# End of a feed-forward and entry of an attention mixer, taken in three token groups

## The chip, the cores and the metric

The kernel runs on one core of one Trainium2 chip. The metric is device time in microseconds (us) of one launch; less is better. Before the change three runs took 2756.0, 2763.02 and 2762.65 us, median 2762.65.

A core has five engines with queues of their own: TensorE (PE in the profile; PEld is its loading of weights), VectorE (DVE), ScalarE (ACT), GpSimd (POOL) and SyncE (SP), which here issues the transfers.

## The reference

Two layers, each a half feed-forward, a token mixer and another half feed-forward, over 512 latent tokens and 256 context tokens of width 1024. Every sub-layer modulates its input and closes with a layer norm of the weighted sum:

```python
def ffn_sublayer(h, shift, scale, gate, w_in, w_out, g, b):
    a, v = jnp.split(modulate(h, shift, scale) @ w_in, 2, axis=-1)
    return layer_norm(ALPHA * h + FFN_RES * gate * ((jax.nn.silu(a) * v) @ w_out), g, b)
# layer 1: first feed-forward (1a), then mixer 1 on u = modulate(h)
qkv = u_lat @ w_qkv                    # 16 query heads, 4 key and 4 value heads of 64
q, k = axial_rope(q) * scale, axial_rope(k)     # latent tokens only
kc, vc = u_ctx @ w_qkv[:, dq:]         # context: keys and values, no rotation
# softmax over a band of +-128 tokens, all context keys and a sink logit per head
```

Latent and context tokens have modulation vectors of their own. In layer 1 the context's output is not needed after mixer 1's keys and values.

## The kernel before

**Layout.** Activations are kept transposed: eight tiles (d = 0..7) of 128 features by 768 tokens, columns 0 to 511 latent (`NL`), 512 to 767 context. `z` is the residual, `uh` and `ul` are the modulated input as a high and a low part, so that a product of near single precision is three matmuls: `mm3` (L162) does high x high, low x high and high x low. Weights are loaded as 256 KB quarters of a unit (`wunit`, L122), and split likewise: the high part by an ACT cast (L102), the low part by a POOL subtraction (L104). They lie in a ring of eight pairs of tiles (`RING`), a unit taking four; the feed-forward's last downs lie in slabs of their own.

**Norms.** `ln` (L1303) makes a list of steps for one group of tokens: `sums`, `mean`, `centers`, `variance`, `spreading`, `out` and `kept`. The first three add the eight tiles on VectorE and POOL, have TensorE take the mean over features, subtract it (L364), square on ACT and add again; `variance` and `spreading` compute the reciprocal root (L354 to L359) and spread it over the partitions with TensorE. `out` (`mods`, L484) normalises each tile (L480) and modulates it in `mod_out` (L299): ACT writes `uf` (L317), ACT or VectorE writes the high part `uh` (L319, L321), VectorE subtracts for `ul` (L322). `kept` (`keep`, L324) scales `z` for the residual on POOL (L329, L335). The latent tokens lie in column order of the grid until a norm with `rm=True` writes them in row order; that was `l3`, the norm behind 1a, whose high part, low part and kept tile go through permuted views.

**Order.** A norm's steps are called at named points of other work: `plan(point=steps)` files them, and `at(point)` in the loops runs them there. That is the order of the program; the framework (`schedule_with_timeline_sim=True`, L1511) then fixes each engine's own order when the kernel is built, by what a simulated timeline has ready. `behind(x, y)` adds an order by hand.

**End of 1a** (`ffn`, from L786). `av` is an up product: a and v, 48 matmuls for a group of tokens, then silu, product and split (L522 to L525). `down` adds eight tiles of 48 matmuls to `z` (L495). The last unit's products go: latent up, latent down of the unit before, latent up, latent down; then the same for the context (256 columns), with the latents' norm beside it; the context's norm only begins at the end.

**Entry of mixer 1** (`wa_mixer`, L1103). Values of four latent token tiles (`v_tiles`, L872, tile vw), keys (wk), each rotated by `rope` (a matmul with a rotation matrix, prk, and three elementwise operations) and stacked in halves by `stack_k` (L859); then queries (wq, prq) for the first two head groups, the context's keys (wkc), and the context's values, for which the values' weights are loaded a second time (tiles with _b). Meanwhile the context's norm is made. Then the attention: scores (sw, sc), exponentials (pw, pc), transposes (tpw, tpc) and outputs (wo).

## Time and profile before

| | |
|---|---|
| profiled execution, its own time | 2773.53 us |
| its span | 2771.7 us |
| mean granted TensorE clock | 0.985 |
| TensorE (PE) busy | 96% |
| VectorE (DVE) / ScalarE (ACT) / GpSimd (POOL) busy | 67% / 43% / 60% |
| read from HBM | 300.92 MB, 113 GB/s over the span with what is written |

How to read the rows below. A row of busy time by stretches has the stretch, its length, then for PE, PEld, DVE, ACT and POOL the busy time with the number of instructions, then the granted TensorE clock (1.00 is full), the share of the DMA engines and GB/s. A row of waits names who waited for whom: total us, times, longest. A row of instructions has its start, its duration, engine, line, operation, what it writes and reads, the shapes and how many were merged; brackets hold the idle time before it and what ended it. A row of groups has the count behind x, then the busy time and the mean of one in ns, then idle time before. TensorE overlaps its matmuls, and their ends are modelled, so the distance of starts is its pace.

### The profile page before, as it was taken

Reading aid. Unit: us, or ns where it says so; the run is one execution under the profiler, and the core shown is the slowest. Engines: PE = TensorE matmul, PEld = TensorE weight load, DVE = VectorE, ACT = ScalarE, POOL = GpSimd, SP = SyncE. Lnnn points to the kernel's source line nnn. Section 1 sums busy time; section 2 is a strip of 40 time slices with the busy share of each in tenths; the row PEclk is TensorE's granted clock in tenths of the full one; section 3 lists DMA queues with packets and bytes.
Section 4 is the critical chain, followed back from the end, with each engine's and each line's share of the span. In section 5 each row is a group of like instructions: output and inputs, shape, how many; then the busy total and the mean of one; then the engine's idle time right before and its main releaser. Section 6 shows DMA issues by size and latency. Waiting matters only on the chain. (4 is left out here: it accounts for less than half of the span.)

```text
span 2771.7 us, 47917 instructions
## 1 busy us (share of the span) xinstructions
PE 2659.9 (96%) x16954; PEld 2423.5 (87%) x16954; DVE 1857.4 (67%) x4250; ACT 1204.9 (43%) x2493; POOL 1674.3 (60%) x1522
## 2 busy tenths in 40 slices
PE   8999999999999989999999999999998999899997
PEld 5899998888888889999998899999986777898997
DVE  4877777775555677656565776666587667677765
ACT  5334343366446344343433434343336655444442
POOL 4786765464434556867664577767545445667762
PEclk9999999999999999999999999999998999999998
DMA  9367555422222213444453236465722111235551
GB/s 320 105 174 205 143 155 152 144 80 61 58 58 57 63 46 92 117 127 126 125 132 106 73 87 165 112 166 165 205 87 63 32 31 47 63 103 126 133 143 57
DMA packets 295615, 311.92 MB, mean 113 GB/s; under 512 B 27856, under 2 KB 193872, under 8 KB 294352
## 3 DMA queue, kind: packets, MB, share of 16 engines
q1 hardware_dynamic: 278960, 279.36, 33.8%
q0 software_dynamic: 16128, 29.37, 6.3%
q8 instruction: 134, 2.20, 0.3%
q14 instruction: 105, 0.86, 0.1%
q10 hardware_dynamic: 288, 0.14, 0.0%
HBM read 300.92 MB, written 12.25 MB: 113 GB/s over the span
## 5 line engine op out<-in xcount | busy, mean ns | idle before, releaser
L104 POOL TENSOR_TENSOR wl<-wr,wh 128x512 fp32r<-128x512 f32 x200 | 262.7, 1332 | 161.2 <-ACT wh L102 102.7
L104 POOL TENSOR_TENSOR wl_s<-S,wh_s 128x512 fp32r<-128x512 f32 x240 | 316.6, 1354 | 53.5 <-ACT wh_s L102 53.0
L102 ACT CAST wh_s<-S 128x512 fp32r<-128x512 f32 x256 | 155.9, 620 | 430.3 <-POOL S L636 151.2
L636 POOL TENSOR_TENSOR S<-wr,wr 128x512 f32<-128x512 f32 x128 | 173.6, 1356 | 191.8 <-DMA wr<-in_wst_dram 177.5
L211 DVE CUSTOM_DVE_ANT_0 jk<-wt,cb 128x512 f32<-128x512 f32 x360 | 244.5, 679 | 23.7 <-DMA wt<-in_wmodt_dram 18.9
L104 POOL TENSOR_TENSOR wl_a<-wr,wh_a 128x512 fp32r<-128x512 f32 x144 | 189.5, 1364 | 17.9 <-ACT wh_a L102 14.0
L102 ACT CAST wh_a<-wr 128x512 fp32r<-128x512 f32 x192 | 118.9, 622 | 152.8 <-PE pd1b L165 21.8
L102 ACT CAST wh<-wr 128x512 fp32r<-128x512 f32 x200 | 120.3, 617 | 85.5 <-DMA wr<-in_wst_dram 21.9
L495 DVE SCALAR_TENSOR_TENSOR z<-pd0b,gt,z 128x256 f32<-128x256 f32 (+1 forms) x168 | 97.0, 594 | 43.9 <-PE pd0b L166 43.2
L495 DVE SCALAR_TENSOR_TENSOR z<-pd1a,gt,z 128x512 f32<-128x512 f32 (+1 forms) x160 | 95.5, 613 | 39.1 <-PE pd1a L166 38.5
L912 POOL TENSOR_SCALAR p<-p,l 128x512 f32<-128x512 f32 x64 | 44.5, 697 | 110.0 <-DVE l L1020 107.5
L495 DVE SCALAR_TENSOR_TENSOR z<-pd0a,gt,z 128x512 f32<-128x512 f32 (+1 forms) x160 | 93.4, 611 | 16.5 <-PE pd0a L166 16.3
L335 POOL TENSOR_SCALAR z<-z,ag_None,ab_None 128x256 f32<-128x256 f32 (+1 forms) x78 | 62.7, 807 | 63.7 <-DVE uh L321 48.8
L636 POOL TENSOR_TENSOR S<-wr,S 128x512 f32<-128x512 f32 x64 | 90.4, 1413 | 3.5
L636 POOL TENSOR_TENSOR S<-S,wr 128x512 f32<-128x512 f32 x64 | 90.3, 1411 | 2.9
L912 POOL TENSOR_SCALAR pw<-pw,l 128x512 f32<-128x512 f32 (+1 forms) x64 | 41.2, 643 | 66.7 <-DVE l L1214 25.7
L1019 ACT ACTIVATE p<-s,m 128x512 f32<-128x512 f32 x64 | 44.0, 689 | 81.2 <-DVE m L1017 76.5
L317 ACT ACTIVATE ufl<-z,bi_None,sc_None 128x256 f32<-128x256 f32 (+1 forms) x86 | 55.3, 654 | 52.9 <-DVE z L480 51.8
L322 DVE TENSOR_TENSOR ul<-ufl,uh 128x256 fp32r<-128x256 f32 (+1 forms) x88 | 61.0, 699 | 5.1 <-ACT uh L319 3.6
L495 DVE SCALAR_TENSOR_TENSOR z<-pd1b,gt,z 128x512 f32<-128x512 f32 (+1 forms) x91 | 53.2, 618 | 11.2 <-PE pd1b L166 10.4
L211 DVE CUSTOM_DVE_ANT_0 jk<-zspare,cb 128x512 f32<-128x512 f32 x88 | 59.7, 678 | 0.5
L163 PE MATMUL vn<-wh,uh 128*128 128x256 f32 x192 | 54.9, 286 | 1.0 <-DVE nq L856 0.5
(1483 smaller groups left out, 10650.8 us busy)
## 6 DMA issues: line engine op xcount, KB each, us to landing
wr<-in_wst_dram SPq DMA_DIRECT2D x456, 256.0 KB
wt<-in_wmodt_dram SPq DMA_DIRECT2D x206, 256.0 KB
zspare<-in_wmodt_dram SPq DMA_DIRECT2D x50, 256.0 KB
wr_0b<-in_wst_dram SPq DMA_DIRECT2D x47, 256.0 KB
wr_1b<-in_wst_dram SPq DMA_DIRECT2D x47, 256.0 KB
wr_2b<-in_wst_dram SPq DMA_DIRECT2D x47, 256.0 KB
wr_3b<-in_wst_dram SPq DMA_DIRECT2D x47, 256.0 KB
wm<-in_wmod_dram SPq DMA_DIRECT2D x8, 1024.0 KB
```

The costliest lines, as they stand in the source:

```text
L102: nc.scalar.copy(hi[:], src[:])
L104: x = eng.tensor_tensor(out=lo[:], in0=src[:], in1=hi[:].bitcast(F32), op=ALU.subtract)
L163: behind(nc.tensor.matmul(ps, a[0], b[0], start=first, stop=False), in_front[0])
L211: x = nc.vector.tensor_tensor_reduce(out=junk[:], in0=w[:], in1=cb[st], scale=1.0, scalar=0.0, op0=ALU.mult, op1=ALU.add, accum_out=out[st])
L317: nc.scalar.activation(uf[:, :n], zs, AF.Identity, scale=s1, bias=s2)
L322: return hi, nc.vector.tensor_tensor(out=lo, in0=uv, in1=uo.bitcast(F32), op=ALU.subtract)
L335: nc.gpsimd.tensor_scalar(out=zs, in0=zs, scalar1=prm[2][:, d:d + 1], scalar2=prm[3][:, d:d + 1], op0=ALU.mult, op1=ALU.add)
L495: last[0] = nc.vector.scalar_tensor_tensor(out=zt(d, c0, c1), in0=pd, scalar=gt[:, d, st:st + 1], in1=zt(d, c0, c1), op0=ALU.mult, op1=ALU ...
L636: nc.gpsimd.tensor_tensor(out=t[:], in0=a[:], in1=b[:], op=o)
L912: nc.gpsimd.tensor_scalar(out=p, in0=p, scalar1=r, scalar2=0.0, op0=ALU.mult, op1=ALU.add)
L1019: last_exp[0] = nc.scalar.activation(p[:], ps[:], AF.Exp, bias=m[:, 0:1], scale=-1.0, accum_out=l[:, 0:1])
```

## The change

- The downs and ups at the end of 1a go by three groups, `w3`: context first, then the two halves of the latents (256 columns each). Context up, latent up, context down of the unit before, context up, context's last down; then latent down, latent up, and the latents' last down in two halves. Weights are loaded as before.
- The norm `l3` has three groups of 256 columns. Its steps are planned under the latents' downs, and from there at points named wa in the mixer's entry.
- The mixer's entry makes values and keys tile by tile: for each group and each d the six matmuls of the values and the six of both key tiles, as inputs come. Values of a group share a bank, and so do the context's keys; `opener` lets only the first matmul of a bank start it, with the others ordered behind. The second load of the values' weights is gone. Keys are rotated once all groups are through, between and behind the first two query projections; `rope` is cut in `scaled` and `turned`, and uses a bank of "s" instead of "mm".
- Row order is written by `l2`, the norm before 1a, instead of `l3`, and the tile that it leaves free serves from then on as a buffer for the modulation weights (`spare`); there only `uf` and the kept tile go through permuted views.
- In norms of over 256 columns, and in `l3` and `l4`, ACT writes the high part of all eight tiles as a copy of `uf` (before: five tiles on ACT from `z`, three on VectorE).

```diff
     def mod_out(nm, d, c0, c1, st, prm, rm=False, dd=None):
-        uo, uv, lo, zv = uh[d][:, c0:c1], uf[:, :n], ul[d][:, c0:c1], zs
+        uo, uv, lo = uh[d][:, c0:c1], uf[:, :n], ul[d][:, c0:c1]
         if rm:
-            uo, uv, lo, zv = rowm(uo), rows(uv), rowm(lo), rows(zs)
-        nc.scalar.activation(uf[:, :n], zs, AF.Identity, scale=s1, bias=s2)
-        if nm[:2] == "l4" or d in (1, 2, 4, 5, 7):
-            hi = nc.scalar.activation(uo, zv, AF.Identity, scale=s1, bias=s2)
+            nc.scalar.activation(rowm(uv), rows(zs), AF.Identity, scale=s1, bias=s2)
         else:
-            hi = nc.vector.tensor_scalar(out=uo, in0=zv, scalar1=s1, scalar2=s2, op0=ALU.mult, op1=ALU.add)
+            nc.scalar.activation(uv, zs, AF.Identity, scale=s1, bias=s2)
+        if n > 256 or nm[:2] in ("l3", "l4"):
+            hi = nc.scalar.copy(uo, uv)
+        elif d in (1, 2, 4, 5, 7):
+            hi = nc.scalar.activation(uo, zs, AF.Identity, scale=s1, bias=s2)
+        else:
+            hi = nc.vector.tensor_scalar(out=uo, in0=zs, scalar1=s1, scalar2=s2, op0=ALU.mult, op1=ALU.add)
...
     def ffn(...):
+        if parted:
+            x0, x1, x2 = parted
+            ws = [wunit(again=u)]
+            av(ws[0], "l_0", x0, *gl[0], None, 4)
+            av(ws[0], "l_0", a, *gl[0], None, 4)
+            tick()
+            wd = [wunit("L", again=u - 1)]
+            down(wd[0], f"{NCH - 2}", gs, x0, True)
+            ws.append(wunit(again=u + 1))
+            av(ws[1], "l_1", x0, *gl[1], None, 4)
...
+            wd.append(wunit("L", again=u + 2))
+            down(wd[1], "l", gl, x0, True)
+            for f in post(0):
+                f()
+            down(wd[0], f"{NCH - 2}", gs, a, True)
+            av(ws[1], "l_1", a, *gl[1], None, 4)
+            down(wd[1], "l", gl, x1, True)
+            for f in post(1):
+                f()
+            down(wd[1], "l", gl, x2, True)
+            for f in post(2):
+                f()
+            return
...
     def wa_mixer(gt):
-        iv = wpos[0]
-        vt = v_tiles("w", wunit(), range(4), ("mm", "c"))
-        w = wunit()
...
+        for gi, (c0, c1, _) in enumerate(w3):
+            for k in range(DT):
+                u = [t[k] for t in (uh, ul)]
+                x = None
+                for j in range(2):
+                    x = mm3(vp[gi][:, j * 256:(j + 1) * 256], [t[:, c0 + j * P:c0 + (j + 1) * P] for t in u],
+                            kw(wv, k, 0, 256), k == 0, k == DT - 1 and j == 1, None if k else x)
+                x = None
+                for i in range(2):
+                    x = mm3(kp[i][:, c0:c1] if gi else kc[:, i * NC:(i + 1) * NC], kw(w, k, i * P, i * P + P),
+                            [t[:, c0:c1] for t in u], k == 0, k == DT - 1 and (i == 1 or gi > 0), None if k or gi else x)
+                at(f"wa{gi}_{k}")
...
+            if gi == 0:
+                for i in range(2):
+                    stack_k(*ks[i], NL, NT, kc[:, i * NC:(i + 1) * NC])
+        kes = [scaled(f"k{i}", kp[i], 1.0) for i in range(2)]
...
+        qes = [query(0, wq, 0)]
         for i in range(2):
-            ps = bank("mm", f"wkc{i}")
-            mmk(ps[:, :NC], w, i * P, NL, NT)
-            stack_k(*ks[i], NL, NT, ps[:, :NC])
-        vt += v_tiles("w", wunit(again=iv), range(4, 6), ("mm", "c"))
+            stack_k(*ks[i], 0, NL, turned(f"k{i}", kes[i]))
+        qes.append(query(0, wq, 1))
+        qs = [stacked_q(f"q0_{i}", qes[i]) for i in range(2)]
...
-    l2 = [ln("l2", i, g, 0, 2, 1, 0, "o", firm=i == 0) for i, g in enumerate(g2)]
-    l3 = [ln("l3", i, g, 1, 0, 1, 3, "o", True, firm=i == 0, alone=i == 1) for i, g in enumerate(g2)]
+    l2 = [ln("l2", i, g, 0, 2, 1, 0, "o", True, firm=i == 0) for i, g in enumerate(g2)]
+    w3 = g2[1:] + g1
+    l3 = [ln("l3", i, g, 1, 0, 1, 3, "oto"[i], held=i < 2) for i, g in enumerate(w3)]
...
-    plan(vw_3=l3[1][1:3], wk1=l3[1][3:4], wq0_0=l3[1][4:6] + l3[0][6:] + l3[1][6:])
+    plan(pd1a_9_0_3=l3[0][1:3], pd1a_9_0_7=l3[0][3:4], pa1a_l_1_0=l3[0][4:6], pv1a_l_1_0=l3[0][6:],
+         pd1a_l_256_3=l3[1][1:3], wa0_2=l3[1][3:4], wa0_4=l3[1][4:6], wa0_6=l3[2][1:3],
+         wa1_2=l3[2][3:4], wa1_5=l3[2][4:6], wa1_7=l3[1][6:], wa2_7=l3[2][6:])
```

67 lines of the change are left out of this document (42 added, 25 removed).

## The prediction

> **What bounds the kernel now.** I read the head of the page first, then busy time by stretches around the change, then TensorE's waits there, then single instructions.
>
> ```profile
> span 2771.7 us, 47917 instructions
> PE 2659.9 (96%) x16954; PEld 2423.5 (87%) x16954; DVE 1857.4 (67%) x4250; ACT 1204.9 (43%) x2493; POOL 1674.3 (60%) x1522
> ```
>
> TensorE is busy 96% of the span; only about 112 us are idle in all, so a change of order can win only where TensorE waits, or where its clock is down. The stretches show where that is:
>
> ```profile
> 2060.00:2080.00 20.00, 15.57 (x108) 13.74 (x106) 19.95 (x27) 13.38 (x15) 13.91 (x9) 1.00 0.00 1
> 2080.00:2100.00 20.00, 18.02 (x79) 14.69 (x80) 15.53 (x38) 6.15 (x15) 7.84 (x6) 0.83 0.23 59
> 2100.00:2120.00 20.00, 15.55 (x67) 11.97 (x66) 16.35 (x31) 17.73 (x32) 10.37 (x10) 0.91 0.05 14
> ```
>
> From the end of 1a's downs to the start of mixer 1's attention TensorE has 15 to 18 us of work in each 20, while VectorE is full in the first stretch (19.95 of 20). Who is late, from TensorE's waits between 2064 and 2148 us (the smallest three left out):
>
> ```profile
> PE vw L166 <- DVE ul L322: 4.7, 4, 1.9
> PE prq L1119 <- ACT qeq L1117: 3.9, 1, 3.9
> PE sw L1175 <- ACT pw L1200: 3.0, 3, 1.5
> PE vw L163 <- DVE uh L321: 1.2, 1, 1.2
> PE tpw L893 <- DVE wkl L864: 1.2, 1, 1.2
> PE vw L165 <- POOL wl_2b L104: 1.0, 1, 1.0
> PE vw L165 <- POOL wl_1b L104: 0.6, 1, 0.6
> ```
>
> These make 15.6 us: waits for the latent tokens' modulated tiles (4.7 and 1.2), for the queue of rotations (3.9), for the values' weights loaded a second time (1.6), for the context's stacked keys (1.2), and the filling of the attention (3.0). And the clock fell three times after such waits:
>
> ```profile
> 2082.00:2088.00 6.00, 5.11 (x23) 5.11 (x24) 5.40 (x10) 1.36 (x3) 2.05 (x2) 0.50 0.25 76
> 2109.00:2113.00 4.00, 3.56 (x7) 2.21 (x8) 2.84 (x7) 3.95 (x8) 2.19 (x3) 0.57 0.00 0
> 2140.00:2147.00 7.00, 6.21 (x26) 4.90 (x27) 5.38 (x16) 5.00 (x19) 3.40 (x5) 0.52 0.44 112
> ```
>
> Busy time multiplied by what the clock lacks (5.11 x 0.50, 3.56 x 0.43, 6.21 x 0.48) is 2.6 + 1.5 + 3.0 = 7.1 us. So about 22.7 us are lost between 2064 and 2148; that is the pot.
>
> **What the change does, part by part.** *Narrower matmuls.* The latent half of the last down and the latent keys go in two groups of 256 columns.
>
> ```profile
> 2031.11 0.39 PE L163 MATMUL pd1a_l<-gh1a_l,wh_2b 128*128 128x512 f32 x1
> 2031.34 0.39 PE L165 MATMUL pd1a_l<-gl1a_l,wh_0b 128*128 128x512 f32 x1
> 2050.15 0.28 PE L165 MATMUL pd1a<-gl1a,wh_0b 128*128 128x256 f32 x1
> 2050.27 0.28 PE L166 MATMUL pd1a<-gh1a,wl_0b 128*128 128x256 f32 x1
> ```
>
> What counts is the distance of the starts: 0.226 us at 512 columns (over a long run of rows), 0.12 us at 256. Two halves cost 0.24, so each pair adds 0.014. The down has 8 x 6 = 48 such matmuls and the keys 2 x 24 = 48: 96 pairs, +1.3 us on TensorE, which is the path. The Trainium skill ("TensorE: Matmul & The Clock Gate", Back-to-back issue gap) has a start-to-start of N/2.4 + 2.5 ns; by that a pair would add 2.5 ns and the whole 0.24 us. The trace has about 10 ns more for each matmul, so I keep 1.3.
>
> *Ends of the downs.* Today a whole down of other tokens lies between the last gated tile of 1a and its use. Now the context's last up product is followed at once by the down that reads it, and so is the latents'. The way from the last up matmul to the split tile is four operations:
>
> ```profile
> 2047.41 0.39 ACT L522 ACTIVATE sl1a_l<-pa1a_l 128x256 f32<-128x256 f32 x1
> 2050.23 0.43 DVE L523 TENSOR_TENSOR pv1a_l<-pv1a_l,sl1a_l 128x256 f32<-128x256 f32 x1
> 2011.65 1.33 POOL L104 TENSOR_TENSOR wl_3b<-wr_3b,wh_3b 128x512 fp32r<-128x512 f32 x1
> ```
>
> With the two that follow, of the same size, that is 1.6 us for the context, and (by width) some 2.6 for the latents. The first halves of the sums (i=0, three matmuls of 0.12 each, in the four or so free banks: 1.4 us) cover most of it. I take 0.8 us, ends 0 and 2.5. The weights are there: the last unit's split on POOL ended at 2013 us (third row), and the new order needs it at about 2024. Their loads keep their order on SP's queue; the moved steps issue no others.
>
> *The norm of the latents.* Today it is one norm of 512 columns whose output is permuted to row order while it is split. The same operations at the entry of 1a are not permuted:
>
> ```profile
> L322 DVE TENSOR_TENSOR ul<-ufl,uh 128x512 fp32r<-128x512 f32 x8 | 14.0, 1752 | 0.0
> L319 ACT ACTIVATE uh<-z,bi_None,sc_None 128x512 fp32r<-128x512 f32 x5 | 6.7, 1341 | 0.0
> L329 POOL TENSOR_SCALAR z<-z,ag_None,ab_None 128x512 f32<-128x512 f32 x7 | 13.0, 1851 | 3.0 <-DVE uh L321 2.6
> L322 DVE TENSOR_TENSOR ul<-ufl,uh 128x512 fp32r<-128x512 f32 x8 | 6.7, 838 | 0.0
> L317 ACT ACTIVATE ufl<-z,bi_None,sc_None 128x512 f32<-128x512 f32 x8 | 6.5, 814 | 11.3 <-DVE z L480 11.3
> L335 POOL TENSOR_SCALAR z<-z,ag_None,ab_None 128x512 f32<-128x512 f32 x8 | 9.5, 1198 | 0.0
> L102 ACT CAST wh<-wr 128x512 fp32r<-128x512 f32 x200 | 120.3, 617 | 85.5 <-DMA wr<-in_wst_dram 21.9
> ```
>
> The first three rows are 2060 to 2085, the next three 1534 to 1556, the last the whole span. The lower parts alone take VectorE 14.0 us against 6.7. In the new order the permutation is gone from here and VectorE loses the three high parts too, which is why the first wait (5.9 us) and its slow clock (2.6) should go. Instead there are three small norms. The context's, 256 columns wide today, shows the size:
>
> ```profile
> 2090.46 2.74 DVE L364 TENSOR_TENSOR z<-z,pml 128x256 f32<-128x256 f32 x8 [1.57 <-PE pml L442]
> 2097.65 0.17 DVE L472 TENSOR_SCALAR pvl<-pvl 128x2 f32<-128x2 f32 x1 [0.70 <-PE pvl L467]
> 2108.24 0.75 DVE L480 TENSOR_TENSOR z<-z,prl 128x256 f32<-128x256 f32 x2
> 2058.21 0.17 DVE L472 TENSOR_SCALAR pvl<-pvl 128x4 f32<-128x4 f32 x1 [1.26 <-PE pvl L467]
> 2062.26 1.27 DVE L480 TENSOR_TENSOR z<-z,prl 128x512 f32<-128x512 f32 x2
> L317 ACT ACTIVATE ufl<-z,bi_None,sc_None 128x256 f32<-128x256 f32 x8 | 4.6, 593 | 0.1
> ```
>
> From centring to the root's start are 7.2 us. From there to the first normalised tile it took 10.6 us, but among the rotation's work; the latents' own (fourth and fifth row) took 4.1. A first split tile is then four operations of 0.4 to 0.6 us, 2 us. With 2 us of sums that is 15.5 us. The context's norm lies under the latents' downs and up product (2 x 48 x 0.226 + 2 x 48 x 0.12 = 33 us) and costs nothing; without that cover it would be these 15.5 us. The first latent group's lies under the other group's down (48 x 0.12 = 5.8) and the context's values and keys (96 x 0.12 = 11.5): 17.3 us, hidden with 1.8 to spare. The second group has 11.5 us more cover, but its centering stands behind the first group's output on VectorE and its squares behind it on ACT (8 tiles x two operations of 0.59 = 9.4 us). So it is centred while the first group's tiles are made, starts its additions when they end, and has its first tile some 10 us later, while TensorE needs 11.5 us for the eight tiles: I work out 0 to 4 us of wait and take 2.0; at the far end, 7 (the contended 10.6 in place of 4.1). TensorE's order has the small matmuls of a norm in it, so such a wait holds all that is queued behind it, the keys' matmuls above all.
>
> *Entry of the mixer.* The second load of the values' weights goes (four 256 KB transfers on SP's queue, four casts, four POOL subtractions), with the 1.6 us waited for it; the context's keys are stacked early, which takes the 1.2. But the values' and keys' weights now hold all eight pairs of the ring until the last group, so the query's weights can be split only as that group's tiles pass; the last quarter is needed 4 us behind the group (six tiles x 0.68) and takes about 2 (cast 0.6, POOL 1.3): nothing, if POOL isn't behind with the two keeps; else up to 2. Both query projections (24 x 0.226 = 5.4 us each) now stand before the queries are rotated, and those of the context, today's filler at that point (first and last row below; the third is the attention's first output), are done.
>
> ```profile
> 2117.36 0.28 PE L163 MATMUL vw<-wh_0b,uh 128*128 128x256 f32 x1
> 2134.41 0.28 PE L166 MATMUL vw<-wh_3b,ul 128*128 128x256 f32 x1
> 2147.81 0.44 PE L903 MATMUL wo<-pw,vtw 128*64 128x128 f32 x4
> ```
>
> So after the last query TensorE has nothing but rotations (about 1 us) until one is added and stacked: I take 2.5 us, ends 0 and 6 (ACT's stack of keys and queries in one row). Then the attention fills as today: 3.0 of wait and 3.0 of slow clock stay, ends 2 and 10, since that filler is missing.
>
> *Entry of 1a.* The permutation moves here. ACT makes all eight tiles: a permuted one of 1.34 and a copy of 0.8 or less, with four casts of 0.6 about 19 us in all, against 21.7 us that TensorE needs for the 96 matmuls of 512 that read them. So it stays just ahead. POOL's keeps cost 8 x (1.85 - 1.20) = 5.2 us more, and the context's sums are queued behind them there; VectorE is relieved of three operations. TensorE's waits there today:
>
> ```profile
> PE pa1a L163 <- DVE uh L321: 1.0, 1, 1.0
> PE pa1a L165 <- DVE ul L322: 0.8, 2, 0.6
> ```
>
> I take 1.5 us more, ends -1.8 (they vanish) and +5 (the whole delay of POOL). In the other norms of 512 columns the high part also goes from VectorE to ACT in three tiles of eight: three operations of 0.81 (fifth row of the groups above) change their engine beside TensorE's work. I take nothing; uncovered it would be 2.4 us to either side.
>
> *The sum.* Lost today 22.7 us. Kept or new: 1.3 + 0.8 + 2.0 + 2.5 + 3.0 + 3.0 + 1.5 = 14.1. Left are 8.6, and 0.7 of the small waits that the rows above leave out go too: -9.3 us. The profiled execution took 2773.53 us (1.8 around its span) and becomes 2764.2. The runs shown have their median 0.4% lower, at 2762.65, and 0.4% of nine microseconds is nothing: **2753.4 us**.
>
> **Rivals.** *A, the entry's end takes the gain.* The values' and keys' matmuls were already issued tile by tile as the inputs came (the timeline shows vw and wk by turns from 2065), so only the shorter norms help, and what they win is given back waiting for the stacked queries and in an attention that fills without filler: 6 in place of 2.5, 10 in place of 6, and 4 for the second group. That is 9 us worse: no change, 2762. For it: ACT is busy 17.73 of 20 us at 2100 to 2120 with just these stacks. Against: keys and context are complete earlier, and two of today's three slow stretches come before.
>
> The Trainium skill (same page, The HAM clock gate) says that an idle window of about 3.4 us halves the clock and a busy one of that length restores it. By that rule a wait for the second group of 2 us leaves the clock alone, and only the query's wait with the fill halves it once: my single 3.0. The rows agree in the half (0.50), though 2082 came after three waits of 1.1 to 1.9 us and no whole idle window.
>
> *B, the norms queue one behind the other: slower.* If the second group's centring does not start until the first group's output is through, and each chain takes as long as the context's did (17.8 us from centring to the first normalised tile), then the first group, centred at 2062, has its first split tile at 2082, 4.5 us after TensorE wants it; it ends at 2093.5; the second is centred at 2092 and has its first tile at 2112, 18.5 us late: 23 us lost where I have 2. Against the 9.3 gained that is 12 us slower: 2774.5. It decides from 11 us of waiting before the groups (no gain); from 20 the loss is measurable. For it: VectorE was full (19.95 of 20) in this place with one norm, and now has two chains in a row. Against: ACT's 9.4 us leave VectorE gaps in which the second group can centre.
>
> *C, everything hides.* The queries' rotation is drawn into the second projection and the groups never wait: 2.0 + 2.5 + 3.0 + 1.5 more, -18: 2744.
>
> **How the numbers follow.** About 0.3%, 8 us, is what a measurement of this kernel can tell from no change. Forecast 0.58 (of which 0.44 beyond 8 us and 0.14 inside), A 0.20, B 0.12, C 0.10. Faster 0.44 + 0.10 = 0.54, same 0.14 + 0.20 = 0.34, slower 0.12. The range takes C and the good ends below, A with the entry of 1a at its worst above (+5 or so): 2742 to 2769; B stays out. The forecast's own range is 2746 to 2759.
>
> **What would show it.** Right: no wait of vw for ul above 1 us in the first two groups, no second load of the values' weights, clock at 1.00 until the first scores, the last query matmul near 2117 us and the first wo near 2132 (2147.8 today), lower parts of 0.4 us. The entry of 1a keeps its waits within 3 us, with POOL's keeps at 1.3 to 1.9 us. Wrong: waits above 4 us before a group's first tile (B); or the first wo near 2145 with the gap before it (A); or a loss of over 3 us between 1535 and 1660.

## The result, and the profile after

The changed kernel is slower: ratio to the kernel before 1.0073, 95% interval 1.0048 to 1.0098, which is 20 us (13 to 27) on the 2759.32 us that the kernel before took as median of the runs beside it. The median of the changed kernel's four runs is 2783.99 us.

The profiled execution of the changed kernel is the lowest of its runs (2773.63 us), the one of before lies 14 us above the median of its kernel (2773.53). So the two spans are nearly equal by chance, and the traces have to be compared by stages. First the head of the page after:

```profile
span 2771.8 us, 48164 instructions
PE 2651.6 (96%) x17052; PEld 2423.0 (87%) x17052; DVE 1839.1 (66%) x4282; ACT 1210.4 (44%) x2528; POOL 1668.4 (60%) x1536
```

The stages are cut at four marks of TensorE, the same in all kernels: start of the last down matmul of 0b (pd0b_l), of the last matmul of the background product p61a, which is the last before the changed end of 1a, of the first and of the last attention output of mixer 1 (wo). In us:

```
                    pd0b_l    p61a      first wo  last wo   last prfin
before              1536.42   1993.31   2147.81   2355.04   2759.09
changed             1522.87   1982.40   2148.27   2362.46   2759.08
length before                  456.9     154.5     207.2     404.1
length changed                 459.5     165.9     214.2     396.6
```

The change costs 2.6 us in 1a with its entry, 11.4 at the end of 1a and the mixer's entry, and 7.0 in the attention: 21 us, as the timed runs say. Only these three lengths are used below. Outside them the trace of before is the slower one: it is 13.5 us behind at the first mark, and its 1b takes 404 us, against 395 to 402 in the changed and trial kernels. Of the 13.5, 7.3 arise between the first and the last matmul of the background product p60a in 0a (344.9 us in before, 337.6 in the changed kernel). The change does nothing there, and e3 below, which is the changed kernel in that place, takes 343.5: that is a difference between executions. The rest lies in part where the change acts (the first modulation and the norms of 512 columns ahead of the mark have all high parts from ScalarE too); with one trace of before it stays open whether some of it is a gain of the change. The marks p61a and first wo in the trace of the changed kernel:

```profile
1982.40 0.33 PE L169 MATMUL p61a<-uh,wl_a 128*128 128x384 f32 x1
2148.27 1.09 PE L940 MATMUL wo<-pw,vtw 128*64 128x128 f32 x16
```

The stretches of the changed kernel that answer to those shown of before (columns: stretch, then busy time and count of TensorE, weight loads, VectorE, ScalarE, GpSimd, then granted clock, share and GB/s of the transfers):

```profile
2060.00:2080.00 20.00, 9.93 (x68) 8.93 (x67) 12.72 (x42) 8.78 (x24) 6.76 (x10) 0.78 0.03 7
2080.00:2100.00 20.00, 16.90 (x118) 16.25 (x118) 13.66 (x44) 12.00 (x29) 7.49 (x13) 0.80 0.01 1
2100.00:2120.00 20.00, 19.00 (x122) 16.64 (x121) 8.43 (x15) 10.31 (x23) 15.47 (x15) 1.00 0.38 107
2120.00:2140.00 20.00, 11.81 (x40) 7.78 (x38) 16.32 (x20) 15.04 (x25) 9.67 (x7) 0.73 0.20 52
```

VectorE is relieved, as intended (12.72 in place of 19.95), but TensorE has only 9.93 us of work in the first 20, at a lower clock. What it waits for between 2064 and 2148 us:

```profile
PE pvl L475 <- DVE aql L355: 6.9, 1, 6.9
PE prq L1160 <- ACT qeq L1154: 4.7, 1, 4.7
PE sw L1235 <- ACT pw L1260: 4.5, 2, 2.9
PE vw L164 <- ACT uh L324: 3.0, 1, 3.0
PE pml L450 <- DVE yl L367: 1.8, 1, 1.8
PE prl L403 <- DVE yl L367: 1.3, 1, 1.3
PE wq L164 <- ACT qek L1154: 1.0, 1, 1.0
PE sw L1235 <- DVE wq L893: 0.6, 1, 0.6
```

The first, fourth, fifth and sixth row are one stall, in front of the first latent group's first value matmul: 13.0 us. TensorE's and GpSimd's instructions there, in order of time:

```profile
2054.19 1.09 POOL L343 TENSOR_SCALAR z<-z,ag_None,ab_None 128x256 f32<-128x256 f32 x2 [10.72 <-ACT ufl L322]
2059.40 0.91 POOL L355 TENSOR_TENSOR asl<-zspare,z 128x256 f32<-128x256 f32 x1
2061.24 1.76 POOL L355 TENSOR_TENSOR asl<-asl,z 128x256 f32<-128x256 f32 x2
2066.25 0.59 PE L450 MATMUL pml<-asl,onesd 128*128 128x256 f32 x2
2067.15 0.28 PE L169 MATMUL wkc<-uh,wl 128*128 128x256 f32 x1
2074.37 1.02 PE L475 MATMUL pvl<-onesd,aql 128*128 128x1 f32 x4 [6.94 <-DVE aql L355]
2083.85 0.58 PE L164 MATMUL vw<-wh,uh 128*128 128x256 f32 x1 [2.96 <-ACT uh L324]
```

The group's last accumulation ends at 2048.3 us, its sums (asl) are done at 2063.9, their mean is taken at 2066.3, one microsecond before the context's keys (wkc) end, and almost everything after that is a wait.

### The profile page after: what moved, and what is told of

Read it like the earlier page. It is cut to its first block, busy times and chain, and to the rows that moved or that the text cites. A ratio compares the mean times of both kernels' runs of the same rounds, so it can differ in the third digit from the quotient of the medians.

```text
span 2771.8 us, 48164 instructions
## 1 busy us (share of the span) xinstructions
PE 2651.6 (96%) x17052; PEld 2423.0 (87%) x17052; DVE 1839.1 (66%) x4282; ACT 1210.4 (44%) x2528; POOL 1668.4 (60%) x1536
## 4 chain that ended last, share of the span: by engine, by line
PE 53%; DVE 7%; ACT 2%; DMA 2%; issue 1%; POOL 1%; SPq 0%; DVEq 0%; ACTq 0%; POOLq 0%
PE pd0b L164 2%; PE pd0b L168 2%; PE pd0b L169 2%; PE pd1a L168 2%; PE pd1a L164 2%; PE pd1a L169 2%; PE wo L940 1%; PE pd1b L164 1%; PE pd1b L168 1%; PE pd1b L169 1%; DVE z L503 1%; DMA wr<-in_wst_dram 1%; PE tpw L930 1%; DVE z L372 1%; PE wq L164 0%
## 5 line engine op out<-in xcount | busy, mean ns | idle before, releaser
L503 DVE SCALAR_TENSOR_TENSOR z<-pd1a,gt,z 128x512 f32<-128x512 f32 (+1 forms) x150 | 88.0, 606 | 34.1 <-PE pd1a L169 26.8
L343 POOL TENSOR_SCALAR z<-z,ag_None,ab_None 128x256 f32<-128x256 f32 (+1 forms) x84 | 57.0, 682 | 68.6 <-DVE uh L328 36.8
L168 PE MATMUL vn<-wl,uh 128*128 128x256 f32 x192 | 54.3, 283 | 0.0
```

Source lines behind the costliest of these rows:

```text
L168: nc.tensor.matmul(ps, a[0], b[1], start=False, stop=False)
L343: nc.gpsimd.tensor_scalar(out=zs, in0=zs, scalar1=prm[2][:, d:d + 1], scalar2=prm[3][:, d:d + 1], op0=ALU.mult, op1=ALU.add)
L503: last[0] = nc.vector.scalar_tensor_tensor(out=zt(d, c0, c1), in0=pd, scalar=gt[:, d, st:st + 1], in1=zt(d, c0, c1), op0=ALU.mult, op1=ALU ...
```

## The experiments

Stage lengths less those of before (456.9, 154.5 and 207.2), and the timed ratios with their intervals:

```
kernel                                 1a     to first wo  attention  ratio
changed                               +2.6    +11.4        +7.0       1.0073 [1.0048, 1.0098]
e1  no scaling of the context         +2.6     +6.5        +8.3       1.0037 [1.0019, 1.0055]
e2  context's norm earlier            +2.1    +11.6        +6.6       1.0055 [1.0040, 1.0069]
e3  rotation in its former bank       +1.8    +11.0        +0.8       1.0034 [1.0017, 1.0051]
e4  row order alone (on before)       +2.3     -8.4        +0.5       0.9982 [0.9962, 1.0001]
e5  own buffer for the sums           +1.9     +7.6        +8.1       1.0021 [1.0008, 1.0034]
e6  five places mended                +1.9     +8.0        -0.3       1.0023 [1.0008, 1.0038]
e7  row order alone, highs shared     +4.2     -9.0        +0.2       0.9942 [0.9923, 0.9960]
e8  earlier and own buffer            +3.3    +11.1        +2.1       1.0035 [1.0017, 1.0054]
e9  as e4, again                      +2.8     -8.3        +0.2       0.9956 [0.9942, 0.9971]
e10 no context norm                   +4.2     -2.7        +9.1       1.0022 [1.0008, 1.0036]
e11 e4, first query scaled on VectorE +2.9    -10.5        +0.1       0.9972 [0.9957, 0.9988]
e12 e10, bank, later centring         +3.7     +2.8        +1.8       1.0028 [1.0016, 1.0041]
```

e4 and e9 are the same kernel, and their lengths differ by 0.5 us at most. The lengths of 1a differ more, from +1.8 to +4.2, among kernels in which it is the same. All of them hang on the one trace of before, and for most kernels they add up to more than the timed loss: in e5 to 17.6 us, where the ratio says 6, in e1 to 17.4 for 10; e9 gains 5.3 us by the lengths and 12 by the ratio. So several microseconds lie outside the three stages, as said above, and a ratio does not confirm a length by itself.

Four theories of the 13 us were tried: GpSimd's order (1), too much work on VectorE and ScalarE (2), ScalarE's stacking between the squares (3), and, from e1 on, the buffer of the sums (4).

**e1.** The context's kept tiles leave the plan:

```diff
-    plan(pd1a_9_0_3=l3[0][1:3], pd1a_9_0_7=l3[0][3:4], pa1a_l_1_0=l3[0][4:6], pv1a_l_1_0=l3[0][6:],
+    plan(pd1a_9_0_3=l3[0][1:3], pd1a_9_0_7=l3[0][3:4], pa1a_l_1_0=l3[0][4:6],
```

> The changed kernel without the eight operations on POOL that scale the context's residual after its norm (left out of the computation: the context's residual keeps its unscaled value; nothing on the path waits for it). Theory 1 (POOL, in its order, has these eight ahead of the sums of the first latent group's norm, so that the sums wait until about 2063 us though their inputs are there at about 2050): the sums come about 8 us earlier, the mean matmul of the first latent group at about 2058 instead of 2066, the 13 us of waits before its first tile fall to 3 to 5 us, the first wo comes near 2139 instead of 2148.3, and the time is 8 to 10 us below the changed kernel's, level with the kernel before within 3 us. Theory 2 (VectorE and ScalarE have too much to do there, whatever the order): the first wo stays within 2 us of 2148. Theory 3 (ScalarE's stacking of the context's keys stands between the squares of the norm): the mean matmul comes early, but the first tile by less than 4 us earlier, since the wait for the variance grows instead.

Measured: first wo 4.9 us better. But the sums, with GpSimd empty, still began late, and the mean came only 0.9 us earlier by the marks (this trace runs 6.3 us ahead at p61a), the group's first value 1.4; the other 3.5 us were gained behind the queries' rotation. The first of the sums, and the mean:

```profile
2050.58 0.74 POOL L355 TENSOR_TENSOR asl<-zspare,z 128x256 f32<-128x256 f32 x1 [13.40 <-DVE ul L329]
2059.02 0.59 PE L450 MATMUL pml<-asl,onesd 128*128 128x256 f32 x2
```

GpSimd idles for 13.4 us and is released by a lower part (ul) of the context, of which the sums read nothing. It is the ring: `total` takes its two tiles from the six buffers of `t2`, which the context's eight unsplit tiles (`uf`) hold since the change, because they no longer have the buffers of the mixer's phase. Theory 1 is wrong in the size that it gave; theory 4 follows, and e5 tests it.

**e2.** Mean of the context's norm ahead of the next product, root and output at earlier points:

```diff
...
+            if firm == 2:
+                in_front[0] = x
...
-    plan(pd1a_9_0_3=l3[0][1:3], pd1a_9_0_7=l3[0][3:4], pa1a_l_1_0=l3[0][4:6], pv1a_l_1_0=l3[0][6:],
+    plan(pd1a_9_0_5=l3[0][1:3], pa1a_l_1_0=l3[0][3:4], pv1a_l_1_0=l3[0][4:],
```

> The changed kernel with the context's norm drawn forward: its mean matmul stands ahead of the next product of the latents' downs, and its root and its output are put one or two plan points earlier. Theory 1 (the context's norm is drawn out from 2020 to 2054 us by its place in TensorE's order and by being mixed with the latents' downs, and its operations on POOL then delay the first latent group): the context's mean matmul at about 2026 instead of 2032, POOL's scaling of the context over by about 2055 instead of 2061, waits before the first group's first tile 13 to about 7 us, first wo near 2142. Theory 2 (too much work on VectorE and ScalarE): the first wo stays within 2 us of 2148, the earlier work only comes in the way of the latents' sums. If the sums on VectorE that stand behind the background's products set the mean, the mean matmul stays at about 2030 and the gain is under 3 us.

Measured: nothing gained (+11.6). The context's scale factors were spread 4.8 us earlier (first row below against 2052.38 in the changed kernel, with the traces 4.8 apart at p61a), but the first group's waits only changed their place:

```profile
2042.78 0.61 PE L403 MATMUL prl<-idn,yl 128*128 128x128 f32 x4
2071.63 1.19 PE L450 MATMUL pml<-asl,onesd 128*128 128x256 f32 x2 [3.06 <-DVE pvl L366]
2077.19 1.20 PE L403 MATMUL prl<-idn,yl 128*128 128x128 f32 x4 [4.37 <-DVE yl L367]
```

**e3.** One word:

```diff
-            pr = bank("s", f"pr{nm}")
+            pr = bank("mm", f"pr{nm}")
```

> The changed kernel, with the queries' rotation again in a bank of the ring that it had before (one word). If the three waits of 1.87 us for an attention output's split at 2196, 2255 and 2312 us, which only the changed kernel has, come from the bank, they go: 4 to 6 us less between 2150 and 2370, and the wait of 4.7 us for the rotated query stays. If they come from the order of the rotation among the heads, nothing moves by more than 2 us. It may also hold the rotations of the first query behind the values' banks: up to 3 us more before the first wo.

Measured: the attention's loss falls from 7.0 to 0.8 us. The wait between 2160 and 2370 us that only the kernels with the rotation in the other bank have (changed kernel), and the longest one of this run there:

```profile
PE pow L164 <- DVE z L503: 5.6, 3, 1.9
```

```profile
PE pa1b L164 <- ACT uh L324: 2.8, 1, 2.8
```

So the bank that the rotation takes sets, in these kernels, the order of the output projection (pow) among the heads: in the changed kernel it begins ahead of the second rotation of a pair (pow at 2185 us, prq at 2186), in e3 behind it (prq at 2187, pow at 2188), as in the kernel before. It is a part of the change that the prediction did not price at all.

**e4 and e9.** The kernel before, with the permutation moved to `l2` and ScalarE making the high parts, and nothing else of the change (the lines of `mod_out` and `spare` are the change's):

```diff
...
-    l2 = [ln("l2", i, g, 0, 2, 1, 0, "o", firm=i == 0) for i, g in enumerate(g2)]
-    l3 = [ln("l3", i, g, 1, 0, 1, 3, "o", True, firm=i == 0, alone=i == 1) for i, g in enumerate(g2)]
+    l2 = [ln("l2", i, g, 0, 2, 1, 0, "o", True, firm=i == 0) for i, g in enumerate(g2)]
+    l3 = [ln("l3", i, g, 1, 0, 1, 3, "o", firm=i == 0, alone=i == 1) for i, g in enumerate(g2)]
```

> The kernel before with one part of the change alone: the permutation to row order moved from the norm behind 1a to the one ahead of it, and the high parts of the wide norms taken by ScalarE as a copy. Nothing else of the change. By the prediction's terms: the entry of 1a loses 1.5 us (2.6 by the trace of the changed kernel), while behind 1a the lower parts take VectorE 0.84 in place of 1.75 us each and the 5.9 us of waits for them with 2.6 us of slow clock shrink to 1 to 2: a gain of 3 to 6 us in all, time near 2755. Rival (VectorE is not what sets those waits, but the norm's own chain): lower parts shorter, waits still above 4 us, and the loss at the entry of 1a stays: 0 to 3 us slower than before.

> The kernel before with the part about the row order alone, with ScalarE making all eight high parts, a second time with more rounds, to be set beside the run in which VectorE makes three of them. By the profiles (1.9 us less at the entry of 1a, 1.4 us less in the whole span) it should be as fast as that one within 0.2%, and 0.4 to 0.6% faster than the kernel before.

Measured: faster than both kernels, by 0.2% (not yet sure) and then 0.4%. Which of the two, the permutation or VectorE's three high parts, gives how much was not taken apart. Behind 1a the wait of 4.7 us for lower parts is gone, that of 1.2 for the first high part is left, and the lower parts take 0.74 us each in place of 1.75; at the entry of 1a ScalarE is 2.8 us late (e9, by groups and waits):

```profile
L326 DVE TENSOR_TENSOR ul<-ufl,uh 128x512 fp32r<-128x512 f32 x8 | 5.9, 736 | 0.0
PE vw L164 <- ACT uh L321: 1.2, 1, 1.2
L164 PE MATMUL pa1a<-uh,wh 128*128 128x512 f32 x16 | 6.4, 402 | 2.8 <-ACT uh L321 2.8
```

**e5.** Theory 4 alone:

```diff
-        accs = [t2(f"{nm}_{i}")[:, :n] for i in range(2)]
+        accs = [ph["L"].tile([P, 256], F32, tag="as", name=nm, bufs=1)[:]] * 2 if nm == "asl3_1" else [t2(f"{nm}_{i}")[:, :n] for i in range(2)]
```

> The changed kernel with one line other: the tile into which the first latent group's sums are added has a buffer of its own, in place of one from the ring of six that it shares with the context's unsplit tiles. Theory 4 (formed on the run without the context's scaling: even with GpSimd free, the sums began only when the context's third lower part had been made, so it is the ring, not GpSimd, that holds them): GpSimd's sums follow at once on the group's last accumulation, at about 2049 us and ahead of the context's scaling, TensorE has the mean's matmul about 8 us earlier, near 2058, and the waits before the group's first tile fall from 13 us to 6 to 8, partly as a new wait of 2 to 3 us ahead of the context's values; first wo 4 to 7 us earlier than the changed kernel's 2148.3 by the same start. Theory 1 (GpSimd's order alone): the sums come no earlier than the context's scaling lets them, nothing moves by over 2 us.

Measured: the sums follow at once, the mean is taken 12 us earlier, before the context's values. Yet the first wo gains only 3.8 us:

```profile
2046.39 0.74 POOL L355 TENSOR_TENSOR asl<-zspare,z 128x256 f32<-128x256 f32 x1 [2.22 <-DVE z L503]
2054.49 0.59 PE L450 MATMUL pml<-asl,onesd 128*128 128x256 f32 x2
2077.94 0.68 PE L403 MATMUL prl<-idn,yl 128*128 128x128 f32 x4 [4.30 <-DVE yl L367]
2081.84 0.58 PE L164 MATMUL vw<-wh,uh 128*128 128x256 f32 x1 [3.22 <-ACT uh L324]
```

From the mean to the first value are now 27.4 us, where the changed kernel has 17.6: centring, squares and sums of the group stand among the output of the context's norm on VectorE, ScalarE and GpSimd, until 2068.0 us. Then the variance waits 3.5 us for its place in TensorE's order (2071.5), and the group's root is mixed with the second group's centring on VectorE (2072.1 to 2077.8). Theory 4 holds for the sums and is not enough for the stall.

**e6.** Own buffer, former bank, the context's keys stacked and its scaling done later, and in the plan:

```diff
...
-         pd1a_l_256_3=l3[1][1:3], wa0_2=l3[1][3:4], wa0_4=l3[1][4:6], wa0_6=l3[2][1:3],
-         wa1_2=l3[2][3:4], wa1_5=l3[2][4:6], wa1_7=l3[1][6:], wa2_7=l3[2][6:])
+         pd1a_l_256_3=l3[1][1:3], wa0_2=l3[1][3:4], wa0_4=l3[1][4:6], wa1_0=l3[2][1:3],
+         wa1_4=l3[2][3:4], wa1_6=l3[2][4:6], wa1_7=l3[1][6:], wa2_7=l3[2][6:])
```

> The changed kernel with every delay mended that the runs so far have shown: own buffer for the first latent group's sums, rotation in its former bank, the context's keys stacked one group later (off ScalarE while the squares are made), the second latent group's mean and centring moved behind the first group's first tile, the context's scaling behind the context's values. If the order of small work is what cost the time (theories 1, 3 and 4 together): waits before the first latent group's first tile 3 to 5 us in place of 13, none over 1 us before the second's, first wo near 2137 by the changed kernel's start, 5 us less in the attention, and 13 to 17 us less than the changed kernel in all: level with the kernel before or up to 6 us faster. If VectorE and ScalarE have too much to do (theory 2): the waits move to the second group and to the stacked keys, the first wo comes no earlier than 2144.

Measured: the attention is repaired, the stall is shorter (2.2 + 3.1 us before the first group), but now the second group waits (1.3 + 1.9), as do the context's first tiles (2.4, in e5 too): +8.0 to the first wo. The stacking stayed where it was: the move in the program did not move it in ScalarE's order. But in e5 and e6 the group's squares are over before the stacking begins (2066.9 and 2073.2 us in e5) and the stall is still there, so theory 3 is a part of it at most. The waits in front of the two groups' first values:

```profile
2075.88 0.58 PE L164 MATMUL vw<-wh,uh 128*128 128x256 f32 x1 [3.10 <-ACT uh L324]
2094.50 0.58 PE L164 MATMUL vw<-wh,uh 128*128 128x256 f32 x1 [1.93 <-ACT uh L324]
```

**e7.** As e4, with three of the eight high parts ahead of 1a copied by VectorE:

```diff
-            hi = nc.scalar.copy(uo, uv)
+            hi = (nc.vector.tensor_copy if nm[:2] == "l2" and d in (0, 3, 6) else nc.scalar.copy)(uo, uv)
```

> The kernel before with the permutation to row order moved to the norm ahead of 1a, as in the run of that part alone, but with three of the eight high parts there copied by VectorE and five by ScalarE, as the kernel before shares them. The loss of 2.3 us at the entry of 1a (one wait of 2.8 us for ScalarE's high parts) should fall to 1 us or less if ScalarE's share sets it; if the permuted operations themselves set it (1.4 us each on ScalarE, 1.1 on VectorE), it stays within 0.5 us of 2.3. Behind 1a it gains 8 us as before. Time 5 to 9 us below the kernel before.

Measured: no gain at the entry of 1a. TensorE waits 1.3 us for a high part and 3.2 for lower parts that VectorE now makes later, in place of 2.8 for a high part; the stage's 4.2 us says little, since the kernels with ScalarE making all eight show 1.8 to 4.2. Its ratio (0.9942) is nevertheless the lowest; in the profiled spans e4, e7, e9 and e11 are within 4.6 us (2747.6, 2749.0, 2750.0, 2745.4), and which of the four is best stays open.

**e8.** e2 and e5 together, former bank, the group's mean put at the end of the latents' last down:

```diff
...
+    plan(pd1a_9_0_5=l3[0][1:3], pa1a_l_1_0=l3[0][3:4], pv1a_l_1_0=l3[0][4:],
+         pd1a_l_256_7=l3[1][1:3], wa0_2=l3[1][3:4], wa0_4=l3[1][4:6], wa1_0=l3[2][1:3],
```

> The changed kernel with the context's norm drawn forward (as in the run of that part), an own buffer for the first latent group's sums, that group's mean matmul put at the end of the latents' last down ahead of the context's values, the second group's mean and centring behind the first group's first tile, and the rotation in its former bank. Each of the two parts alone gained at most 4 us, because the context's norm and output (16 operations on VectorE, 16 on ScalarE, 8 on GpSimd) then still lay between the group's sums and its squares. Theory 1+4 (order): with the context's output over by about 2052 us, before the group's sums are complete, its chain runs free: mean matmul at about 2054, variance near 2062, first tile 0 to 3 us after the end of the context's keys in place of 13; first wo 9 to 13 us earlier than the changed kernel's by the same start, 6 us less in the attention, in all 2748 to 2756 where the kernel before takes 2759. Theory 2 (VectorE and ScalarE have too much to do between 2040 and 2075): the waits only move into the downs and the second group; first wo gains less than 6 us and the time stays above the kernel before's.

Measured: nothing gained to the first wo (+11.1). The context's output still lasted until 2062 us, since VectorE now made it by turns with the latents' accumulations, which came later by it; TensorE waited 4.0 us for the sums at 2063.91, before the context's keys. Here the norm drawn forward delayed what it was put in front of, since each engine's order is fixed when the kernel is built.

**e10.** The context's norm left out, to see what it costs (its values and keys are made from the tiles of the norm before, so the kernel does not compute the reference):

```diff
-    plan(pd1a_9_0_3=l3[0][1:3], pd1a_9_0_7=l3[0][3:4], pa1a_l_1_0=l3[0][4:6], pv1a_l_1_0=l3[0][6:],
-         pd1a_l_256_3=l3[1][1:3], wa0_2=l3[1][3:4], wa0_4=l3[1][4:6], wa0_6=l3[2][1:3],
+    plan(pd1a_l_256_3=l3[1][1:3], wa0_2=l3[1][3:4], wa0_4=l3[1][4:6], wa0_6=l3[2][1:3],
...
```

> The changed kernel without the context's norm behind 1a (left out of the computation: its sums, mean, root, output and scaling; the context's values and keys are made from the modulated tiles of the norm before, which TensorE, and nothing else, reads in the same way). Nothing then stands between the first latent group's accumulations and its norm, neither a buffer, nor work on VectorE, ScalarE or GpSimd. If the context's norm is what delays the group (whatever the resource): sums at about 2052, mean matmul at about 2054 to 2057, first tile 0 to 4 us after the context's keys end, first wo 8 to 12 us earlier than the changed kernel's by the same start. If the group's own chain of small steps is longer than the cover (5 us of sums, 13 to 16 us from the mean to the first split tile against 19 us from the last accumulation to the end of the context's keys), a wait of 4 to 8 us stays although the engines are half empty, and the gain is 3 to 8 us.

Measured: 14.1 us better to the first wo (-2.7 against before), more than either theory gave. Mean at 2055, variance at 2065, and a wait of 4.3 us is left:

```profile
2055.36 0.60 PE L450 MATMUL pml<-asl,onesd 128*128 128x256 f32 x2
2064.66 0.50 PE L475 MATMUL pvl<-onesd,aql 128*128 128x1 f32 x4
2073.52 0.58 PE L164 MATMUL vw<-wh,uh 128*128 128x256 f32 x1 [4.28 <-ACT uh L324]
```

So the context's norm costs this stage 14 us, and in the order that is left the group's own chain is some 4 longer than its cover.

**e11.** e4 with the first query's scaled copy on VectorE:

```diff
+            if nm == "q0_0":
+                nc.vector.tensor_scalar(out=qe[:], in0=ps[:], scalar1=scale, scalar2=None, op0=ALU.mult)
+            else:
+                nc.scalar.activation(qe[:], ps[:], AF.Copy, scale=scale)
```

> The kernel before with the part about the row order alone, and with the scaled copy of the first query made by VectorE, since ScalarE has it behind eleven operations of stacking the keys (the wait of 3.9 us of the first rotation for it is in both). If ScalarE's queue sets that wait, it falls to 1 to 2 us, the first scores come 2 us earlier and the time is 1 to 4 us below that of the row order alone; if it only moves the wait to the stacked query, nothing changes within 1 us.

Measured: the first rotation waits 3.4 us in place of 3.9, now for VectorE, and the stacked query 1.8 in place of 0.4. The stage is 2 us shorter than in e4 and e9, the ratio no better than theirs: no gain that can be told.

**e12.** e10 with the former bank and the second group's centring later:

```diff
...
+    plan(pd1a_l_256_3=l3[1][1:3], wa0_2=l3[1][3:4], wa0_4=l3[1][4:6], wa1_0=l3[2][1:3],
+         wa1_4=l3[2][3:4], wa1_6=l3[2][4:6], wa1_7=l3[1][6:], wa2_7=l3[2][6:])
```

> As the run without the context's norm (left out of the computation as there), and with the rotation in its former bank and the second latent group's mean and centring behind the first group's first tile. The wait of 4.3 us that was left before the first group should fall to 1.5 to 2.5, since VectorE no longer centres the second group (2.65 us) ahead of the first group's output, and the 9 us lost in the attention should fall to 0 or 1. If the two latent norms fit behind one another when nothing else is in their way, the second group then waits 2 us or less and the first wo comes 2 to 4 us earlier than in that run; if they don't fit, the second group waits 3 to 6 us, and the first wo is within 2 us of that run. Time 8 to 14 us below the changed kernel's in either case, from the attention.

Measured: 3.8 us before the first group, 2.3 + 1.9 before the second, and 5.5 us worse to the first wo than e10; the attention's loss falls to 1.8:

```profile
2068.84 0.39 PE L164 MATMUL vw<-wh,uh 128*128 128x256 f32 x1 [3.81 <-ACT uh L324]
2085.53 0.68 PE L403 MATMUL prl<-idn,yl 128*128 128x128 f32 x4 [2.34 <-DVE yl L367]
2088.15 0.58 PE L164 MATMUL vw<-wh,uh 128*128 128x256 f32 x1 [1.93 <-ACT uh L324]
```

In this order the two latent norms don't fit behind one another even when the context's is gone, and not for lack of engines: between 2080 and 2085 us, where the second group's wait begins, VectorE is busy 2.3 us and ScalarE not at all. Against theory 2 stands e5 too, with VectorE busy 12.6 and ScalarE 9.6 of the 18 us from 2054 to 2072. What is full is no engine but the chain as it is ordered. Part of it is standing in line for TensorE. The first group's sums, its summed squares and the small matmuls that read them:

```profile
2048.76 0.41 DVE L355 TENSOR_TENSOR asl<-pml,z 128x256 f32<-128x256 f32 x1
2051.57 0.60 PE L450 MATMUL pml<-asl,onesd 128*128 128x256 f32 x2
2057.73 0.42 DVE L355 TENSOR_TENSOR aql<-pml,sql 128x256 f32<-128x256 f32 x1
2060.87 0.50 PE L475 MATMUL pvl<-onesd,aql 128*128 128x1 f32 x4
```

The mean is taken 2.4 us after its sums are done, the variance 2.7 after its squares, and the root is spread 0.8 after it is ready: 5.9 us for places in TensorE's order, more than the 3.8 that TensorE then waits. Whether earlier places for these three would let the norms fit was not tried.

## Why the prediction was wrong

It forecast a gain of 9.3 us and the change lost 20.

**The context's norm: the step that failed.** The prediction said that it "lies under the latents' downs and up product" for 33 us "and costs nothing". It did lie under them: its first tile came 34 us after its last accumulation, with TensorE waiting 1.0 us. But it took the whole cover in place of the 15.5 us worked out (whose parts add up to 15.3), because its small matmuls stand in TensorE's order behind others (sums done at 2027.3, mean at 2032.0), and its root, of eleven short operations, was spread between accumulations over 6.3 us. In the changed kernel, the sums' last addition, the mean, the first and last operation of the root, and the first value:

```profile
2026.84 0.41 DVE L355 TENSOR_TENSOR asl<-pml,z 128x256 f32<-128x256 f32 x1
2032.01 0.59 PE L450 MATMUL pml<-asl,onesd 128*128 128x256 f32 x2
2043.68 0.16 DVE L480 TENSOR_SCALAR pvl<-pvl 128x2 f32<-128x2 f32 x1
2049.82 0.16 DVE L367 SCALAR_TENSOR_TENSOR yl<-pvl,yl 128x2 f32<-128x2 f32 x1
2054.92 0.39 PE L164 MATMUL vw<-wh,uh 128*128 128x256 f32 x1 [0.98 <-ACT uh L324]
```

And what was hidden from TensorE was not free for the next norm: its output came at 2053 to 2061, where the first latent group's sums (in e5 its squares too) wanted the same engines and, through the ring, the same buffers. e10 gives the price: 14.1 us.

**The first latent group.** What should be "hidden with 1.8 to spare" became 13.0 us of stall. Of the terms, the sums were taken at 2 us, for which the prediction had no row, and took 15.6 (from 2048.3 to 2063.9; in e5, with their own buffer, about 5). From the mean to the first value I had 13.5, measured 17.6, and 18.2 in e10, where nothing of the context is in the way: there the variance and the spreading of the root stand 3.9 us in TensorE's order, and VectorE centres the second group ahead of the first's output. So, as ordered, the chain was some 4 us too long for its cover even without the context.

**The second group.** 2.0 us predicted, 0.1 measured, but only since the first group's stall gave it time; where that is mended (e6, e12) the second waits 3 to 4.

**Queries and filling.** 2.5 us for the stacked query were 5.3 (4.7 and 0.6), 3.0 of filling 4.5, and one of 1.0 for the first query's product is new.

**The clock.** One stretch of 3.0 us was foreseen, and two came, of 17 us each. Busy time multiplied by what the clock lacks (7.55 x 0.50 and 10.89 x 0.50) is 3.8 + 5.4 = 9.2 us. The first stretch is the stall's: it begins in the wait of 6.9 us, and ends 4 us after TensorE has work again.

```profile
2068.00:2071.00 3.00, 0.00 (x0) 0.00 (x0) 2.38 (x7) 2.40 (x8) 2.02 (x3) 1.00 0.00 0
2071.00:2088.00 17.00, 7.55 (x29) 6.51 (x30) 13.93 (x46) 12.39 (x33) 6.17 (x11) 0.50 0.00 1
2129.00:2146.00 17.00, 10.89 (x36) 7.34 (x37) 11.17 (x25) 10.64 (x26) 6.18 (x7) 0.50 0.12 32
```

The Trainium skill ("TensorE: Matmul & The Clock Gate", The HAM clock gate) has about 3.4 us for both ways. The trace is near it: the clock fell 3.6 us after the last matmul's end (2067.4) and was back 4.3 us after the first value's start (2083.9). The prediction's reading of that rule, that a wait of 2 us leaves the clock alone, did not hold in e12: there the clock halved near 2087 us, in the second of two waits of 2.3 and 1.9 us with a few small matmuls between, as the trace of before did after three waits of 1.1 to 1.9.

Against the terms to the first wo these are 13.0 - 1.9 + 2.8 + 1.5 + 1.0 + 6.2 = 22.6 us. The sum had this stage 10.8 us better than before (the gain of 9.3 and the 1.5 of the entry of 1a, which lies outside it), and it was 11.4 worse: 22.2. That the two agree so closely is in part luck: the first two terms (2.1) and the smallest waits are not in the count. The mark that I named for it, first wo near 2132, was 6.5 us more hopeful than my own sum (2147.8 less 9.3).

**What was right.** Narrower matmuls and ends of the downs together were 2.1 us; up to the first value the stage lost 0.8 by the marks. The entry of 1a lost 2.6 in place of 1.5 (1.8 to 4.2 in the twelve kernels that have it), for the reason given: ScalarE's permuted tiles, one wait of 2.8. That the permutation and VectorE together set the old 5.9 us, e4 and e9 show: to the first wo they gain 8.3 us, where waits and slow clock of that place were put at 5.9 + 2.6.

**The bank.** `rope` cut in two "and uses a bank of 's'" stood in the change and had no term. It costs some 7 us of the attention's length (6.6 to 9.1 in the five kernels with it, -0.3 to 2.1 in the eight without). How much of that 1b gives back is open: 1b takes 397 us on average in the five and 399 in the eight, with 395 to 402 among each other.

**The rivals.** B had the place (waits before the groups, norms one behind the other) and the sign, at a chance of 0.12; its own arithmetic put 4.5 us before the first group and 18.5 before the second, the reverse of what came. Its argument, that VectorE would be full, is not what happened: VectorE was busy 12.7 of 20. A had the end of the entry about right (5.3 us for the stacked query where it put 6), but no term for the first group, which is most of the loss. Of C nothing came.

## What to carry to other kernels

Work that is hidden from the critical engine is not free for the next chain: ask which buffers and which places in the other engines' queues it holds, and until when, and price a norm cut in three as three chains of dependent small operations, not as a third of its busy time each, and count the time that its small matmuls stand in TensorE's order. When a tile's operands move to another buffer ring, look who else allocates from that ring: here eight tiles in a ring of six held up sums that had nothing to do with them. And take a large change apart: one of its parts (the row order, with the high parts on ScalarE) was a gain by itself, and the rest cost more than it gave.

## What the runs showed of the hardware that was not expected

VectorE's subtraction for the lower parts reads and writes contiguous columns in the changed kernel, yet it took 1.14 us each at the entry of 1a, beside GpSimd's permuted scaling of 1.74 us, against 0.84 beside the contiguous scaling of 1.20 in the kernel before (quoted in the prediction). By groups, entry of 1a, changed kernel:

```profile
L336 POOL TENSOR_SCALAR z<-z,ag_None,ab_None 128x512 f32<-128x512 f32 x7 | 12.2, 1736 | 0.1
L329 DVE TENSOR_TENSOR ul<-ufl,uh 128x512 fp32r<-128x512 f32 x8 | 9.1, 1140 | 3.2 <-ACT uh L324 3.2
```

Whether the two engines hinder one another there was not tried.
